# Both down projections of a two-layer trunk by seven products instead of eight

## The chip, the cores and the metric

One Trainium2 chip, one of its cores. The metric is the device time of one execution in microseconds; the kernel before was run three times. A profile is one further execution of the program, recorded by the hardware profiler, with a line for each instruction.

## The reference

One inference step of a trunk with two layers: RWKV-7 time mixing and a feed-forward part, then band attention on shared keys and values and a second feed-forward part. There are 1024 tokens of a prompt and 8 x 16 tokens of samples, so 1152 columns, and 1024 features. The change is in the last line of the feed-forward parts:

```python
D_MODEL, D_FF = 1024, 2816

def modulate(h, shift, scale):
    return h * (1.0 + scale[:, None, :]) + shift[:, None, :]

def swiglu(h, w_gate, w_up, w_down):
    return (jax.nn.silu(h @ w_gate) * (h @ w_up)) @ w_down
...
# each sub-layer: shift, scale, gate from silu(c) @ W + b
# h = modulate(rms_norm(x), shift, scale);  x = x + gate * sublayer(h)
```

The result must be good to fp32.

## The kernel before

Everything is stored with features on the 128 partitions and tokens as columns. Columns lie in two parts: part c=0 has 512, part c=1 has 640 (the last 128 of it are the samples). Every fp32 product is made of three matmuls (`mm3`, all matmuls have its line, L143): both operands are split into a high and a low half of type fp32r (`split`: ScalarE makes the high half, L272, VectorE the low one, L273), and high x high, high x low and low x high are added up in PSUM. So each weight or activation tile costs one operation on ScalarE and one on VectorE before TensorE can use it.

The gates (`gate_up`) run over 22 tiles f of 128 hidden features. For a tile, gate and up projection together are a two by two block product (weights: gate and up by the two halves of the 1024 input features; activations: the same halves by the two halves of the columns of each part), which is made with seven products instead of eight (a form of Strassen's scheme). The combined weights are made on GpSimd (`strassen_weights`, L1340 to L1343), the combined activations once per layer. Each product is twelve matmuls of 256 columns and twelve of 320 into a wide PSUM tile (two of them are named S, one PT; they are used in turn). Evictions add the products up: ScalarE copies, VectorE adds from PSUM, and three additions per tile between SBUF tiles on GpSimd (all additions have L1369). L1383 and L1385 then multiply silu(gate) and up: s0 and s1 are the tile's output for the first and second half of the columns of both parts. They are stored to DRAM (`sd`, L1390). The SBUF tiles of these steps (t, x, xin) come from one pool of 11 buffers, "e", through `ev`.

The down projection (in `ffn`) takes 11 pairs p of hidden tiles. For each pair and column part it loads the activations (`h<-sd`, L1411) into a slot of the pool h0 or h1 (14 slots each), splits them, loads and splits the weights (`rq<-in_wd`, L249, into 16 buffers `w`), and makes eight output tiles n; for each, VectorE adds the pair's product to the sum so far (L1436). The last pairs are reordered so that column part 1 ends first. The input x is added with the gate of the modulation (`residual`, L1170, which also serves the attention).

In layer 0 the modulations of the next sub-layers (16 units of four weight tiles) are computed inside the down projection: `step(7)` after each pair takes the generator `ada_steps` seven steps on, each with a load of 128 x 1024 from `wada` (L260) into a slot of h0, and four small matmuls. When a column part is complete, `done` normalizes and splits it (L1558, L1559) for the keys' and values' projection (`kv`), which begins with `nw = 4` output tiles of the keys. All DMAs of these parts are issued by SyncE's queue (SP) in one order.

The order of instructions on each engine is not written by hand. The code is written stage by stage, and a scheduler orders each engine's instructions; `issue_after` holds a group of instructions behind a given one.

Of the kernel before, what the change touches and what calls it, by code (L numbers as in the profile page):

```python
# [76 lines left out]
def prep(i):  # L77
# [68 lines left out]
class Trunk:  # L146
# [54 lines left out]
    def ada_steps(self, units, tag="aux", bufs=1, tile=None):  # L201
# [3 lines left out]
        def load(u, i):  # L205
            w = (tile or self.rawtile)()
            self.wload(w[:, :1024], self.a["wada"][u, i])
            return w
        todo = [(u, i) for u in units for i in range(4)]
        ahead = None  # L210
        for u in units:
            ps = self.bank(tag, bufs)
            for i in range(4):
# [3 lines left out]
                for q in range(4):  # L217
                    mm(nc, ps[32 * q:32 * q + 32, c], self.scT[:, i % 2 * 4 + q, :], w[:, q * 256:q * 256 + 256], i % 2 == 0, i % 2 == 1)
                if i < 3:
                    yield  # L220
            sb = (tile or self.rawtile)()[:, :512]
# [1100 lines left out]
    def strassen_weights(self, l, f, gp=None):  # L1322
# [4 lines left out]
        def put(t):  # L1327
            hi, lo = (self.wq.tile([128, 512], F32R, tag="w", name=self.nm("w"), bufs=16) for _ in range(2))
# [21 lines left out]
    def gate_up(self, sd, B, W, cs):  # L1350
# [17 lines left out]
        def add(eng, out, x, y):  # L1368
            eng.tensor_tensor(out, x, y, ALU.add)  # L1369
# [12 lines left out]
        add(gp, t5, t5, u3)  # L1382
# [3 lines left out]
        for h, s in enumerate((s0, s1)):  # L1386
            for c in cs:
                o, n = 256 * c - n0, (256, 320)[c]
                t0 = 512 * c + n * h
                nc.sync.dma_start(sd[:, t0:t0 + n], s[:, o:o + n])  # L1390

    def ffn(self, l, B, W, part1, xsrc, dst, done):

        nc = self.nc
        sd = [self.dp.tile([128, 2, 1152], F32, name=f"sd{l}_{p}") for p in range(11)]
        self.gate_up(sd[0][:, 0], B, iter(W), (0,))
        for _ in part1:
            pass
        self.gate_up(sd[0][:, 0], B, iter(W), (1,))
        for f in range(1, 22):  # L1400
            self.gate_up(sd[f // 2][:, f % 2], B, self.strassen_weights(l, f, nc.vector if f == 1 else None), (0, 1))
        self.ada = self.ada_steps(range(12, 28), "acc", 1) if l == 0 else iter(())
        gate = 48 * l + 40
        acc, end = {}, iter(())
        act, W = {}, {}

        def begin(p):
            for c in range(2):
                w = (512, 640)[c]
                raw, hi, lo = (self.slot(c, dt)[:, :2 * w].rearrange("p (i t) -> p i t", i=2) for dt in (F32, F32R, F32R))  # L1410
                nc.sync.dma_start(raw, sd[p][:, :, self.cols(c)])  # L1411
                self.split(hi, lo, raw)
                act[p, c] = hi, lo
            W[p] = [self.halves(self.a[f"wd{l}"][f]) for f in (2 * p, 2 * p + 1)]
            self.step(7)

        for p, c in [(p, c) for p in range(9) for c in range(2)] + [(9, 1), (10, 1), (9, 0), (10, 0)]:
                if (p, c) not in act:
                    begin(p)
                if p == 0:  # L1420
                    acc[c] = self.feats(c)
                if p == 10:
                    st = self.sq_open()
                for n in range(8):
                    ns = slice(n % 4 * 128, (n % 4 + 1) * 128)
                    d, parts = self.pz(c)
                    for z, o, m in parts:
                        for i in range(2):
                            wh, wl = W[p][i][n // 4]
                            hi, lo = (act[p, c][h][:, i, o:o + m] for h in range(2))  # L1430
                            self.mm3(z, wh[:, ns], wl[:, ns], hi, lo, i == 0, i == 1)
# [554 lines left out]
```

## Time and profile before

| | us |
|---|---|
| median of 3 runs | 3810.54 |
| lowest, highest | 3801.19, 3811.68 |
| the profiled execution's own time | 3804.49 |
| its span, first to last instruction | 3802.7 |
| mean granted TensorE clock | 0.940 |

| stretch of the profiled execution, us | what runs |
|---|---|
| 0 to 1290 | layer 0's time mixing |
| 1290 to 1799 | layer 0's gates |
| 1776 to 2148 | layer 0's down projection, with the modulations |
| 2143 to 2280 | keys and values |
| to 3030 | attention |
| 3030 to 3520 | layer 1's gates |
| 3520 to the end | layer 1's down projection |

Neighbouring stages overlap. In the views that follow, L is a line of the kernel, "x24" the number of instructions in a group, times are microseconds unless marked ns, and "<-" in brackets names what ended the engine's wait. A table by windows gives for each stretch its length, then busy time and count of each engine, the granted clock, the busy share of the 16 DMA engines and GB/s.

### The profile page before, as it was taken

Reading aid. Unit: us, or ns where it says so; the run is one execution under the profiler, and the core shown is the slowest. Engines: PE = TensorE matmul, PEld = TensorE weight load, DVE = VectorE, ACT = ScalarE, POOL = GpSimd, SP = SyncE. Lnnn points to the kernel's source line nnn. Section 1 sums busy time; section 2 is a strip of 40 time slices with the busy share of each in tenths; the row PEclk is TensorE's granted clock in tenths of the full one; section 3 lists DMA queues with packets and bytes.
Section 4 is the critical chain, followed back from the end, with each engine's and each line's share of the span. In section 5 each row is a group of like instructions: output and inputs, shape, how many; then the busy total and the mean of one; then the engine's idle time right before and its main releaser. Section 6 shows DMA issues by size and latency. Waiting matters only on the chain.

```text
span 3802.7 us, 72100 instructions
## 1 busy us (share of the span) xinstructions
PE 3506.1 (92%) x28550; PEld 3098.0 (81%) x28550; DVE 2263.6 (60%) x4396; ACT 1573.8 (41%) x3006; POOL 591.6 (16%) x497
## 2 busy tenths in 40 slices
PE   5889989989999799999999899789889799999999
PEld 4777778777667699999888879667677799999898
DVE  4666667765445854554457742666565755545667
ACT  5545546544223533333311452556554533333310
POOL 0000000000011154453000100000000255444000
PEclk9887899899699899999999999899899899999999
DMA  5876776776665322224654122554565322222521
GB/s 212 236 216 170 207 220 184 201 203 201 192 197 176 113 84 76 76 73 157 221 177 172 64 71 92 153 151 155 152 203 178 120 78 71 76 75 96 171 86 66
DMA packets 426995, 554.01 MB, mean 146 GB/s; under 512 B 128385, under 2 KB 292737, under 8 KB 422177
## 3 DMA queue, kind: packets, MB, share of 16 engines
q1 hardware_dynamic: 351344, 450.68, 36.9%
q0 software_dynamic: 22224, 80.36, 6.9%
q10 hardware_dynamic: 53088, 18.36, 2.1%
q8 instruction: 225, 3.69, 0.4%
q14 instruction: 114, 0.93, 0.1%
HBM read 415.85 MB, written 133.40 MB: 144 GB/s over the span
## 4 chain that ended last, share of the span: by engine, by line
PE 69%; DMA 11%; DVE 10%; issue 4%; ACT 4%; SPq 1%; ACTq 0%; POOL 0%; DVEq 0%; POOLq 0%
PE S L143 32%; PE PT L143 15%; PE acc L143 12%; PE st L143 3%; PE O L143 2%; PE G L143 1%; DVE h L273 1%; PE aux L143 1%; PE PT L1811 1%; PE Y L143 1%; DMA TT<-Z 1%; DMA h<-out_kT 1%; DVE wlo L273 1%; DMA raw<-in_rw_o 1%; DMA h<-in_wo 1%
## 5 line engine op out<-in xcount | busy, mean ns | idle before, releaser
L143 PE MATMUL S<-h,w 128*128 128x320 f32 (+1 forms) x4944 | 689.7, 298 | 12.3 <-ACT h L272 4.8
L143 PEld LDWEIGHTS S<-h,w 128*128 128x128 f32 x4944 | 671.8, 191 | 18.4 <-ACT h L272 5.6
L143 PE MATMUL S<-h,wh 128*128 128x320 f32 (+1 forms) x2844 | 529.8, 338 | 15.9 <-DVE h L1170 6.8
L143 PE MATMUL acc<-mx,whi 128*128 128x384 f32 x1728 | 508.5, 372 | 32.7 <-ACT whi L272 13.0
L143 PEld LDWEIGHTS S<-h,wh 128*128 128x128 f32 x2844 | 456.1, 189 | 70.8 <-issue 12.3
L272 ACT ACTIVATE w<-rq 128x512 fp32r<-128x512 f32 x308 | 192.6, 629 | 515.1 <-PE S L143 201.1
L143 PEld LDWEIGHTS acc<-mx,whi 128*128 128x128 f32 x1728 | 337.6, 204 | 63.3 <-ACT whi L272 16.9
L273 DVE TENSOR_TENSOR w<-rq,w 128x512 fp32r<-128x512 f32 x308 | 267.8, 872 | 199.8 <-ACT w L272 199.0
L143 PE MATMUL PT<-h,w 128*128 128x320 f32 (+1 forms) x2448 | 347.6, 297 | 10.2 <-ACT h L272 4.7
L143 PEld LDWEIGHTS PT<-h,w 128*128 128x128 f32 x2448 | 332.1, 190 | 12.2 <-ACT h L272 5.1
L143 PE MATMUL acc<-mx,wlo 128*128 128x384 f32 x864 | 316.1, 366 | 8.3 <-DVE wlo L273 8.3
L1369 POOL TENSOR_TENSOR t<-t,t 128x576 f32<-128x576 f32 (+1 forms) x132 | 226.5, 1717 | 442.2 <-ACT t L1376 320.1
L143 PE MATMUL PT<-h,wh 128*128 128x320 f32 (+1 forms) x1428 | 284.2, 342 | 8.2 <-ACT h L1558 2.3
L143 PEld LDWEIGHTS PT<-h,wh 128*128 128x128 f32 x1428 | 231.7, 188 | 38.5 <-issue 5.0
L143 PEld LDWEIGHTS acc<-mx,wlo 128*128 128x128 f32 x864 | 175.0, 203 | 20.6 <-DVE wlo L273 12.9
L273 DVE TENSOR_TENSOR wlo<-raw,whi 128x1024 fp32r<-128x1024 f32 x114 | 139.1, 1221 | 84.9 <-ACT whi L272 83.8
L272 ACT ACTIVATE wh<-rq 128x512 fp32r<-128x512 f32 x124 | 74.8, 625 | 245.1 <-PE S L143 161.4
L273 DVE TENSOR_TENSOR h<-h,h 128x1024 fp32r<-128x1024 f32 (+4 forms) x112 | 122.3, 1106 | 88.3 <-ACT h L272 72.1
L272 ACT ACTIVATE whi<-raw 128x1024 fp32r<-128x1024 f32 x114 | 119.6, 1053 | 129.0 <-PE acc L143 62.6
L272 ACT ACTIVATE h<-h 128x1024 fp32r<-128x1024 f32 (+4 forms) x112 | 103.5, 935 | 159.8 <-DMA h<-sd 111.1
L1369 DVE TENSOR_TENSOR t<-S,t 128x576 f32<-128x576 f32 (+1 forms) x116 | 86.4, 744 | 122.7 <-PE S L143 122.7
L1436 DVE TENSOR_TENSOR h<-h,S 128x640 f32<-128x640 f32 (+1 forms) x150 | 111.9, 750 | 78.9 <-PE S L143 78.7
(444 smaller groups left out, 5625.0 us busy)
## 6 DMA issues: line engine op xcount, KB each, us to landing
h<-in_wada SPq DMA_DIRECT2D x64, 512.0 KB, 6.3
rq<-in_wg SPq DMA_DIRECT2D x88, 256.0 KB, 2.6
rq<-in_wu SPq DMA_DIRECT2D x88, 256.0 KB, 2.6
rq<-in_wd SPq DMA_DIRECT2D x88, 256.0 KB, 3.1
raw<-in_wada POOLq DMA_DIRECT2D x32, 512.0 KB, 5.0
kc<-in_ck SPq DMA_DIRECT2D x16, 1024.0 KB, 5.1
vc<-in_cv SPq DMA_DIRECT2D x16, 1024.0 KB, 6.0
sd<-t SPq DMA_DIRECT2D x88, 160.0 KB, 1.9
```

The lines of the kernel that those rows point to most:

```text
L143: return nc.tensor.matmul(out, lhsT, rhs, start=start, stop=stop)
L272: self.nc.scalar.activation(hi, x, AF.Copy)
L273: self.nc.vector.tensor_tensor(lo, x, hi, ALU.subtract)
L1369: eng.tensor_tensor(out, x, y, ALU.add)
L1436: nc.vector.tensor_tensor(y, y, d, ALU.add)
L1811: nc.tensor.transpose(pt[:, j * 128:(j + 1) * 128], P[:, j * 128:(j + 1) * 128], self.C("ident"))
```

## The change

The down projection becomes a two by two block product as well, made of seven products. Its four blocks of weights are pairs of (even or odd hidden tiles) and (first or second half of the output features); those of the activations are (even or odd hidden tiles) and (first or second half of a part's columns).

- *Operands.* `down_open` gives `gate_up` a function that stores a tile's s0 and s1. At an even tile s0 is stored and both are kept; at an odd one four operations of VectorE (L1441, L1443, L1445, L1448) make the combinations, and the seven operands of the pair are stored in 14 DMAs (L1418), by product i and group j of four, four and three pairs (`Bd`).
- *Weights.* `down_sums` makes four combined blocks of weights for 1408 columns of each of four output tiles m: 32 groups per layer, one or two per hidden tile, each one load (L1458), four operations of GpSimd on 128 x 176 (L1460 to L1463) and one store (L1464). These four are held behind the gates' last addition on GpSimd (`last_add`).
- *Products.* `down` takes the products in the order 0, 1, 2, 4, 5, then 6 and 3; in layer 0 these last two come first for column part 1 and then for part 0. For each product it loads three operands per column part (L1491) and splits them; for each m it loads three pieces of weights (L1502) and makes 11 x 3 matmuls of 256 columns and as many of 320. PSUM is emptied by ScalarE's copy or VectorE's addition (L1536) into four sums, and residuals, stores and squares follow as soon as an output is complete.
- *Modulations.* A weight tile is loaded as two of 128 x 512 (`aw`, L264) from the pool e; three steps follow each m.
- *Buffers.* The weights have 14 buffers instead of 16, and the keys' projection begins with three output tiles instead of four.

```diff
-            d[f"wd{l}"] = i["w_down"][l].reshape(22, 128, 1024)
+            d[f"wd{l}"] = i["w_down"][l].reshape(11, 2, 128, 2, 4, 128).transpose(2, 3, 1, 4, 0, 5).reshape(128, 4, 5632)
...
-            self.wload(w[:, :1024], self.a["wada"][u, i])
+            n = 1024 // len(w)
+            for j, t in enumerate(w):
+                self.wload(t, self.a["wada"][u, i][:, j * n:(j + 1) * n])
...
-        self.hw = ("w", "w", 16)
+        self.hw = ("w", "w", 14)
...
-            add(gp, t5, t5, u3)
+            self.last_add = add(gp, t5, t5, u3)
...
+    def down_open(self, l):
...
+        def put(p, i, t):
+            for c in range(2):
+                nc.sync.dma_start(self.Bd[c][i][p // 4][:, p % 4], t[:, part[c]])
...
+                put(p, 2, s1)
+                nc.vector.tensor_tensor(t6, s1, e1, ALU.subtract)
+                put(p, 6, t6)
+                nc.vector.tensor_tensor(e1, e1, e0, ALU.subtract)
+                put(p, 4, e1)
+                nc.vector.tensor_tensor(e0, e0, t6, ALU.add)
+                put(p, 5, e0)
+                put(p, 1, s0)
+                nc.vector.tensor_tensor(t3, s0, e0, ALU.subtract)
+                put(p, 3, t3)
...
+    def down_sums(self, l, g):
+        m, j = divmod(g, 8)
+        q = self.wq.tile([128, 4, 176], F32, tag="ws", name=self.nm("ws"), bufs=2)
+        nc.sync.dma_start(q, self.a[f"wd{l}"][:, :, g * 176:(g + 1) * 176])
+        with self.tc.issue_after(self.last_add.ins):
+            gp.tensor_tensor(q[:, 3], q[:, 2], q[:, 3], ALU.add)
+            gp.tensor_tensor(q[:, 2], q[:, 0], q[:, 2], ALU.subtract)
+            gp.tensor_tensor(q[:, 0], q[:, 3], q[:, 0], ALU.subtract)
+            gp.tensor_tensor(q[:, 1], q[:, 1], q[:, 0], ALU.subtract)
+        nc.sync.dma_start(self.Ws[m][:, :, j * 176:(j + 1) * 176], q)
+
+    def down(self, l, xsrc, dst, done):
+        ks = [(j, k) for j, n in enumerate((4, 4, 3)) for k in range(n)]
+        turns = [(i, (0, 1)) for i in (0, 1, 2, 4, 5)]
+        if l:
+            turns += [(i, (0, 1)) for i in (6, 3)]
+        else:
+            turns += [(i, (c,)) for c in (1, 0) for i in (6, 3)]
+            part512 = lambda: self.ev("aw")[:, 0:512]
+            self.ada = self.ada_steps(range(12, 28), "acc", 1, lambda: (part512(), part512()), part512)
...
+        for i, cs in turns:
+            X = operand(i, cs)
+            for m in range(4):
+                W = weights(i, m)
+                d = self.wide()[:, 256:832]
+                for c in cs:
+                    for n, (j, k) in enumerate(ks):
+                        self.mm3(d[:, part[c]], W[j][0][:, s], W[j][1][:, s], hi, lo, n == 0, n == 10)
...
+                self.step(3)
...
-        nw = 4
+        nw = 3
```

SyncE's queue in layer 0's down projection, where the second pair's (before) and the second product's (after) activations are loaded. Here h is a slot for activations, rq a raw tile of weights, aw a modulation tile. Before:

```order
L249 DMA rq_20341<-in_wd 128x512
L249 DMA rq_20347<-in_wd 128x512
L1411 DMA h_19789<-sd_1_14100 128x2x640
L249 DMA rq_20353<-in_wd 128x512
L249 DMA rq_20604<-in_wd 128x512
L1411 DMA h_20059<-sd_2_14101 128x2x640
L260 DMA h_19865<-in_wada 128x1024
```

After:

```order
L1502 DMA rq_20716<-in_wd 128x512
L1502 DMA rq_20722<-in_wd 128x512
L1491 DMA h_20425<-bd_0_1_0_14102 128x1024
L1491 DMA h_20443<-bd_1_1_0_14123 128x1280
L264 DMA aw_20299<-in_wada 128x512
L264 DMA aw_20300<-in_wada 128x512
L264 DMA aw_20394<-in_wada 128x512
```

The modulations' loads are now twice as many, half as large, and stand in the same queue between the operands' groups.

GpSimd in the gates, from the additions of one tile to the next tile's combined weights; t are eviction tiles, ws the down projection's weights. Before:

```order
L1369 TENSOR_TENSOR t_14712<-t_14712,t_14713 128x576
L1369 TENSOR_TENSOR t_14712<-t_14712,t_14714 128x576
L1369 TENSOR_TENSOR t_14713<-t_14713,t_14715 128x576
L1340 TENSOR_TENSOR rq_15265<-rq_15200,rq_15202 128x512
L1341 TENSOR_TENSOR rq_15200<-rq_15196,rq_15200 128x512
```

After:

```order
L1373 TENSOR_TENSOR t_14774<-t_14774,t_14775 128x576
L1373 TENSOR_TENSOR t_14774<-t_14774,t_14776 128x576
L1373 TENSOR_TENSOR t_14775<-t_14775,t_14777 128x576
L1460 TENSOR_TENSOR ws_15010<-ws_15010 128x176
L1460 TENSOR_TENSOR ws_15017<-ws_15017 128x176
L1461 TENSOR_TENSOR ws_15010<-ws_15010 128x176
L1461 TENSOR_TENSOR ws_15017<-ws_15017 128x176
L1462 TENSOR_TENSOR ws_15010<-ws_15010 128x176
L1462 TENSOR_TENSOR ws_15017<-ws_15017 128x176
L1344 TENSOR_TENSOR rq_15360<-rq_15295,rq_15297 128x512
```

Four or eight sums come between the last addition and the combined weights, and some of them later among these.

VectorE at the end of a tile's evictions, after an odd tile in the new kernel; L273 (now L277) is a weight's low half. Before:

```order
L1369 TENSOR_TENSOR t_15435<-PT_15607,t_15434 128x576
L273 TENSOR_TENSOR w_15876<-rq_15682,w_15875 128x512
L1383 TENSOR_TENSOR t_15432<-t_15432,t_15433 128x576
L1369 TENSOR_TENSOR t_15435<-S_15639,t_15435 128x576
L273 TENSOR_TENSOR w_15925<-rq_15916,w_15924 128x512
L1385 TENSOR_TENSOR t_15431<-t_15431,t_15435 128x576
L273 TENSOR_TENSOR w_15955<-rq_15918,w_15954 128x512
L1369 TENSOR_TENSOR t_15671<-PT_15718,t_15670 128x576
```

After:

```order
L1387 TENSOR_TENSOR t_15539<-t_15539,t_15540 128x576
L1373 TENSOR_TENSOR t_15542<-S_15746,t_15542 128x576
L1441 TENSOR_TENSOR t_15773<-t_15539,t_15287 128x576
L277 TENSOR_TENSOR w_16004<-rq_15810,w_16003 128x512
L1389 TENSOR_TENSOR t_15538<-t_15538,t_15542 128x576
L1443 TENSOR_TENSOR t_15287<-t_15287,t_15286 128x576
L1445 TENSOR_TENSOR t_15286<-t_15286,t_15773 128x576
L277 TENSOR_TENSOR w_16065<-rq_16056,w_16064 128x512
L1448 TENSOR_TENSOR t_15774<-t_15538,t_15286 128x576
L1373 TENSOR_TENSOR t_15799<-PT_15846,t_15798 128x576
```

The four operations stand between the last eviction of the odd tile and the next tile's addition from PT.

More of the change, by code (lines that the diff above doesn't have):

```diff
@@ L1327, in put @@
         def put(t):
-            hi, lo = (self.wq.tile([128, 512], F32R, tag="w", name=self.nm("w"), bufs=16) for _ in range(2))
+            hi, lo = (self.wq.tile([128, 512], F32R, tag="w", name=self.nm("w"), bufs=self.hw[2]) for _ in range(2))
             self.split(hi, lo, t)
@@ L1348, in strassen_weights, with gate_up @@
         yield put(a22)
-    def gate_up(self, sd, B, W, cs):
+    def gate_up(self, put, B, W, cs):
         nc = self.nc
@@ L1368, in add @@
         def add(eng, out, x, y):
-            eng.tensor_tensor(out, x, y, ALU.add)
+            return eng.tensor_tensor(out, x, y, ALU.add)
         t1, s0, s1, t5, u2, u3 = (new() for _ in range(6))
@@ L1385, in gate_up @@
         dve.tensor_tensor(s0, s0, u3, ALU.mult)
[L1386 to L1390, printed above, removed]
+        put(s0, s1, cs)
     def ffn(self, l, B, W, part1, xsrc, dst, done):
         nc = self.nc
-        sd = [self.dp.tile([128, 2, 1152], F32, name=f"sd{l}_{p}") for p in range(11)]
-        self.gate_up(sd[0][:, 0], B, iter(W), (0,))
+        spill = self.down_open(l)
@@ new lines, in ffn, with first, even, f @@
+            self.gate_up(spill(f), B, self.strassen_weights(l, f, nc.vector if f == 1 else None), (0, 1))
+            for g in range(32 * (f - 1) // 21, 32 * f // 21):
+                self.down_sums(l, g)
+        return self.down(l, xsrc, dst, done)
+    def down_open(self, l):
+        nc = self.nc
+        part = (slice(0, 256), slice(256, 576))
+        self.Bd = [[[self.dp.tile([128, n, (256, 320)[c]], F32, name=f"bd{l}_{c}_{i}_{j}") for j, n in enumerate((4, 4, 3))] for i in range(7)]
+                   for c in range(2)]
+        self.Ws = [self.dp.tile([128, 4, 1408], F32, name=f"ws{l}_{m}") for m in range(4)]
+        b12 = self.dp.tile([128, 576], F32, name=f"b12_{l}")
+        held = []
+        def put(p, i, t):
+            for c in range(2):
+                nc.sync.dma_start(self.Bd[c][i][p // 4][:, p % 4], t[:, part[c]])
+        def first(s0, s1, cs):
+            c, = cs
+            nc.sync.dma_start(self.Bd[c][0][0][:, 0], s0)
+            nc.sync.dma_start(b12[:, part[c]], s1)
+        def even(p):
+            def f(s0, s1, cs):
+                put(p, 0, s0)
+                held[:] = s0, s1
+            return f
+        def odd(p):
+            def f(s0, s1, cs):
+                if p == 0:
+                    held[:] = (self.ev("t")[:, 0:576] for _ in range(2))
+                    for c in range(2):
+                        nc.sync.dma_start(held[0][:, part[c]], self.Bd[c][0][0][:, 0])
+                    nc.sync.dma_start(held[1], b12)
+                e0, e1 = held
+                t6, t3 = (self.ev("t")[:, 0:576] for _ in range(2))
+                put(p, 2, s1)
[8 more added lines that the diff above has]
+                put(p, 3, t3)
+            return f
+        return lambda f: first if f == 0 else (odd if f % 2 else even)(f // 2)
@@ L1447, in ffn @@
                     next(end, None)
-                if p == 10:
-                    for _ in end:
+            if l == 0 and i == 3:
+                for g in (self.ada, end):
+                    for _ in g:
                         pass
-                    end = done(c, acc[c], st)
+                end = done(cs[0], acc[cs[0]], sq[cs[0]])
         return end
@@ L1489, in weights @@
                         yield
-                for _ in part(0, lambda: self.wq.tile([128, 512], F32, tag="w", name=self.nm("x"), bufs=16)):
+                for _ in part(0, lambda: self.wq.tile([128, 512], F32, tag="w", name=self.nm("x"), bufs=self.hw[2])):
                     pass
```

132 lines of the change are left out of this document (86 added, 46 removed).

## The prediction

> **What bounds the kernel now.** I read the page's sums, the chain that ended last, then a table by stage of both feed-forward parts.
>
> ```profile
> PE 3506.1 (92%) x28550; PEld 3098.0 (81%) x28550; DVE 2263.6 (60%) x4396; ACT 1573.8 (41%) x3006; POOL 591.6 (16%) x497
> PE 69%; DMA 11%; DVE 10%; issue 4%; ACT 4%; SPq 1%; ACTq 0%; POOL 0%; DVEq 0%; POOLq 0%
> core 0: us, PE busy (x) PEld busy (x) DVE busy (x) ACT busy (x) POOL busy (x), PEclk, DMA share, GB/s
> 1290.00:1776.00 486.00, 478.33 (x3539) 475.09 (x3540) 268.59 (x361) 171.10 (x296) 230.21 (x146) 0.99 0.23 77
> 1776.00:1830.00 54.00, 54.00 (x386) 48.06 (x385) 16.22 (x23) 25.03 (x38) 4.61 (x3) 1.00 0.83 298
> 1830.00:1980.00 150.00, 150.00 (x1008) 122.22 (x1007) 84.16 (x117) 30.66 (x39) 0.00 (x0) 1.00 0.56 197
> 2126.00:2170.00 44.00, 34.54 (x165) 29.04 (x164) 37.10 (x73) 19.73 (x41) 7.66 (x5) 0.92 0.19 70
> 3030.00:3520.00 490.00, 485.83 (x3610) 483.95 (x3611) 265.37 (x333) 167.05 (x286) 233.92 (x148) 0.99 0.24 81
> 3600.00:3700.00 100.00, 100.00 (x575) 91.52 (x574) 66.01 (x88) 17.53 (x23) 0.00 (x0) 1.00 0.25 81
> ```
>
> Gates run at 1290–1776 and 3030–3520, the down projections at 1776–2126 and from 3520 to the end. Inside a down projection TensorE leaves no gap (150.00 of 150, 100.00 of 100) at clock 1.00: fewer columns shorten it one for one, as long as loads (0.56 of the DMA engines in layer 0, 0.25 in layer 1) and evictions keep up. In the gates TensorE has 98–99%, so what is added there on VectorE or GpSimd is free only while no eviction comes late.
>
> **Removed: TensorE columns.** Timelines of a down projection and of a gate tile give the price of a matmul from one group's start to the next.
>
> ```profile
> 1500.17 3.36 PE L143 MATMUL PT<-h,w 128*128 128x256 f32 x24
> 1503.37 6.55 PE L143 MATMUL S<-h,w 128*128 128x256 f32 x48
> 3614.97 1.92 PE L143 MATMUL PT<-h,wh 128*128 128x320 f32 x12
> 3616.72 3.68 PE L143 MATMUL S<-h,wh 128*128 128x320 f32 x24
> 3624.76 1.52 PE L143 MATMUL PT<-h,wh 128*128 128x512 f32 x6
> 3626.14 3.06 PE L143 MATMUL S<-h,wh 128*128 128x512 f32 x12
> ```
>
> 320 columns cost 1.75/12 = 0.146 us, 512 cost 1.38/6 = 0.230. A gate product is twelve of 256 and twelve of 320 columns in 3.20 us, 0.133 on average. Before, a layer's down projection has 22 feature tiles x 8 outputs x 3 = 528 matmuls of 512 and 1056 of 320: 121.4 + 154.2 = 275.6 us. After, 7 products x 4 output tiles x 11 x 3 = 924 of 256 and 924 of 320, the gates' mix: 1848 x 0.133 = 245.8. Saved 29.8 a layer, about **-60** in both. The modulations' matmuls are the same in number.
>
> **Layer 0: the loads get closer.** DMA views of 1776–2126 and, for its queue and the operand loads, 3520–3800; then two short windows.
>
> ```profile
> DMA packets 26169, 66.95 MB, mean 191 GB/s; under 512 B 2592, under 2 KB 3616, under 8 KB 26144
> q1 hardware_dynamic: 26144, 66.59, 53.7%
> h<-in_wada SPq DMA_DIRECT2D x64, 512.0 KB, 6.3
> q1 hardware_dynamic: 14807, 29.43, 31.6%
> h<-sd SPq DMA_DIRECT2D x10, 640.0 KB, 4.4
> 1780.00:1820.00 40.00, 40.00 (x287) 34.11 (x286) 12.11 (x16) 17.96 (x27) 4.61 (x3) 1.00 0.96 351
> 1780.00:1790.00 10.00, 10.00 (x77) 10.00 (x76) 5.28 (x6) 5.66 (x8) 1.07 (x1) 1.00 0.98 361
> ```
>
> A packet took 0.537 x 16 x 350 / 26144 = 115 ns at 2.55 KB, and 0.316 x 16 x 280 / 14807 = 96 ns at 1.99 KB: a line of 27 ns + 0.035 ns per byte, so 98 ns for 2 KB, 169 for 4 KB, 62 for 1 KB (estimates). The modulations' 64 loads of 4 KB rows become 128 of 2 KB: 33.6 MB, 16384 packets, 100 us of all 16 engines instead of 87. From the first of them to the last I count besides 17 MB of weights (52 us), 19 MB of operands (49) and 5 MB of x (19): 220 us of all engines. On TensorE this stretch holds the first five products and part of the sixth, 175–180 us, and the modulations' matmuls, 50–55: 228 us. Before, 0.56 was asked of the engines; now 0.96. That share was held for 40 us at a time (0.96), and 0.83 over 54 us. At 0.97 nothing stalls, at 0.83 the stretch lasts 265 us (+37), at 0.75 it lasts 293 (+65). I take 0.89, between the two rows: 247, **+20**; ends 0 and +65. Splitting those loads also doubles their issues on SP (64 more, from a queue in which operand and weight loads stand behind loads that wait for a pool buffer); of the 11 buffers there, x tiles and squares use the same.
>
> The Trainium skill, "DMA: Bandwidth & Descriptors", section "Measured", asks for transfers of 1 MiB for 75% of peak, which speaks against halving these to 256 KB. The trace shows 0.98 and 361 GB/s with transfers of 128 to 640 KB mixed, so here it is many in flight that decide. By that page's limit of about 358 GB/s on the HBM side (section "Where 436 GB/s comes from") the stretch's 74.7 MB would need 209 us, an estimate, and the term would be 0.
>
> **Layer 1** has 20 MB of weights, 23 of operands and 9 of x in 246 us: 213 GB/s, about 0.6. Its price is the start of a product: nine of ten free slots hold the running product's operands, so the next one's second and third load wait for the last output tile's matmuls, then 4.4 us of landing and two splits. With the first group of loads already there and the scheduler taking three output tiles turn about, I take 0.8 us for each of six starts: **+5** (0 to +20), in layer 0 it lies inside the stretch above.
>
> **Gates: four subtractions per two tiles on VectorE, 32 groups of four sums per layer on GpSimd.** Timeline of a tile, and one line's groups.
>
> ```profile
> 1506.23 1.30 POOL L1340 TENSOR_TENSOR rq<-rq,rq 128x512 f32<-128x512 f32 x1
> 1506.30 1.83 DVE L1383 TENSOR_TENSOR t<-t,t 128x576 f32<-128x576 f32 x1 [1.32 <-POOL t L1369]
> 1507.60 1.69 POOL L1341 TENSOR_TENSOR rq<-rq,rq 128x512 f32<-128x512 f32 x1
> 1509.76 0.74 DVE L1385 TENSOR_TENSOR t<-t,t 128x576 f32<-128x576 f32 x1
> 1509.98 1.68 POOL L1342 TENSOR_TENSOR rq<-rq,rq 128x512 f32<-128x512 f32 x1 [0.69 <-DVE w L273]
> 1510.52 1.68 DVE L273 TENSOR_TENSOR w<-rq,w 128x512 fp32r<-128x512 f32 x1
> 1516.92 0.69 DVE L273 TENSOR_TENSOR w<-rq,w 128x512 fp32r<-128x512 f32 x1 [1.91 <-ACT w L272]
> 1520.70 1.42 POOL L1369 TENSOR_TENSOR t<-t,t 128x576 f32<-128x576 f32 x1 [7.08 <-ACT t L1376]
> L1369 POOL TENSOR_TENSOR rq<-rq,rq x6: 852/1515/2327, 1300.0 to 3031.9; 128x256 f32<-128x256 f32 x6
> ```
>
> VectorE's and GpSimd's operations on two SBUF tiles don't overlap: L1383 started at 1506.30, GpSimd ended at 1507.53, L1383 0.60 later (1.83 instead of 0.74); L1342 and the split at 1510.52 show it both ways. A subtraction of 576 columns is 0.74; a sum of 176 columns, from 852 ns at 256 and 1.30 us at 512, about 0.71 (estimate). In two tiles (44.7 us) that adds 4 x 0.74 + 12.2 x 0.71 = 11.6 us, to 14 splits of 0.69, 4 products of 0.74, 6 additions of 1.42 and 8 combinations of 1.30 = 31.5: 43.1 of 44.7. Counting only what an operation still took once released (0.54, 0.60, 1.16), it is some 36. So there is room, but little; GpSimd's idle 7.08 us takes the sums. VectorE's row at the end of an odd tile is four subtractions longer, with two splits between, ahead of the eviction of the next tile's second product; I lay it out to end at 12.4–13.0 us after the tile's start, TensorE wants the bank at 12.8. I take 0.45 us per two tiles, 22 times: **+10** (0 to +45). Weights are prepared some 20 us ahead; 14 buffers instead of 16 cost 3 of these: nothing alone.
>
> The Trainium skill, "SBUF — State Buffer", section "Who interferes with whom", makes this a lock between GpSimd and a VectorE operation with two SBUF inputs; by it the sum is 43 of 44.7, near the point where the gates pay, and the rows above agree.
>
> The 14 stores per two tiles replace 8 (0.23 of the engines busy there): hidden.
>
> **Ends.** Before, TensorE stands twice for VectorE's residuals and splits at layer 0's end:
>
> ```profile
> 2132.50 1.66 PE L143 MATMUL S<-h,wh 128*128 128x512 f32 x6 [2.51 <-DVE h L1170]
> 2140.87 2.41 PE L143 MATMUL S<-h,wh 128*128 128x512 f32 x6 [3.72 <-DVE h L1170]
> ```
>
> After, VectorE still has more work than TensorE between the two column parts (the window at 2126 has it at 37.10 of 44), so the wait of about 10 us stays; the keys' first three output tiles ahead instead of four leave 24 x 2 matmuls of 320 less to fill it, 7 us, of which the fourth's, loaded later, may still fill some: **+3** (0 to +7). The very last output tile has residual, store: **+1** (-2 to +4).
>
> **Sum:** -60 + 20 + 5 + 10 + 3 + 1 = -21 against the profiled execution's own 3804.5 (span 3802.7): 3783.5. The shown median, 3810.5, lies 6 above that execution, the runs from 3801 to 3812; I give a quarter of it: **3785**. What a measurement of this kernel can't tell from no change is 0.3%, 11.4 us.
>
> **Rivals.**
> 1. *All is hidden.* Layer 0's loads hold 0.97 (the window of 40 us speaks for it, the 54 us against), gates and starts cost under 10 in all: -60 + 10 = -50, 3755 to 3765. 0.16.
> 2. *Given back in the gates.* The lock's queueing makes evictions late by 0.9–1.9 us per two tiles (for it: 43.1 of 44.7; against it: 7.08 us of GpSimd idle), +20 to +42: -11 to +11, 3800–3822, about 3808. 0.20.
> 3. *Slower: layer 0's transfers bound it.* With the other terms at -41, it is lost by over 11.4 when the stretch passes 280 us, a share under 0.785; small rows, spills landing and buffers returned late make 0.72 (the 54 us at 0.83 had larger rows): 305 us, +77, in all +36, about 3845. Against it: 351 GB/s over 40 us. 0.16.
>
> **How the numbers follow.** The forecast, a gain of 12 to 42 (3768–3798), has 0.48. Faster 0.48 + 0.16 = 0.64; same 0.20; slower 0.16. The range takes rival 2 whole and most of rival 1: 3750 to 3822.
>
> **What would show it.** Right: down projections of about 246 us in layer 1 from the first product to the last, some 20 longer in layer 0 beyond the modulations' matmuls, DMA share near 0.9 there, TensorE's waits put down to loads of weights or operands; gates of 488–492 us, with some idle time before a second product's first matmul. Wrong: gates over 500 us with TensorE released by VectorE's evictions (rival 2); a layer-0 stretch of 280 us or more (rival 3); share of 0.96 and no waits (rival 1); or a matmul price in the long runs of one PSUM tile other than 0.133.

## The result, and the profile after

The changed kernel's median is 3787.3 us (3780.2 to 3793.9, six runs) against 3806.5 for the kernel before (3801.2 to 3821.9, six runs): ratio 0.9945, interval 0.9929 to 0.9960. The forecast was 3785. The profiled execution of the changed kernel has a span of 3783.6 us; that of before had 3802.7.

First the page's sums and its chain that ended last; then the table by windows, with the columns of the prediction's table. Its rows are 440 us of the gates in either layer, layer 0's stretch with the modulations, that layer's down projection as a whole, its end, and three pieces of layer 1's down projection: its first four output tiles (the first product), the next seven, and the last seventeen with the tail (a tile is 66 matmuls).

```profile
PE 3457.2 (91%) x29078; PEld 3088.6 (82%) x29078; DVE 2248.3 (59%) x4380; ACT 1667.9 (44%) x3182; POOL 769.7 (20%) x743
PE 65%; DMA 13%; DVE 10%; issue 6%; ACT 4%; SPq 1%; POOL 1%; ACTq 0%; DVEq 0%; POOLq 0%
...
1360.00:1800.00 440.00, 440.00 (x3310) 440.00 (x3309) 258.13 (x297) 144.33 (x238) 299.53 (x253) 1.00 0.46 147
3060.00:3500.00 440.00, 440.00 (x3309) 440.00 (x3308) 260.26 (x298) 142.95 (x237) 307.72 (x258) 1.00 0.45 143
1822.70:2078.00 255.30, 252.48 (x2018) 217.11 (x2016) 120.67 (x208) 99.51 (x161) 0.00 (x0) 1.00 0.86 297
1807.30:2285.70 478.40, 453.18 (x3191) 392.18 (x3190) 255.04 (x466) 213.52 (x390) 9.76 (x9) 0.98 0.62 210
2097.00:2165.00 68.00, 56.51 (x366) 52.35 (x366) 50.67 (x117) 34.11 (x70) 0.00 (x0) 0.90 0.39 121
3518.20:3554.60 36.40, 35.47 (x265) 35.06 (x263) 18.18 (x21) 10.33 (x20) 10.57 (x9) 1.00 0.77 252
3554.60:3629.20 74.60, 66.93 (x463) 65.79 (x463) 37.88 (x53) 31.71 (x45) 0.00 (x0) 0.93 0.66 219
3629.20:3783.60 154.40, 149.68 (x1124) 149.42 (x1122) 84.86 (x155) 49.49 (x77) 0.00 (x0) 1.00 0.50 160
```

TensorE works 48.9 us less (3506.1 to 3457.2), not 60. The gates take every microsecond of TensorE (440.00 of 440) although GpSimd is busy for 300 us of it. Where TensorE stands or runs slower is in layer 0's down projection and in the second and third product of layer 1's (66.93 busy of 74.60, granted clock 0.93, for seven tiles).

For before, the row of the whole down projection of layer 0, from its first matmul to the values' projection that follows:

```profile
1797.30:2289.60 492.30, 474.14 (x2927) 395.11 (x2926) 288.39 (x489) 159.99 (x280) 15.74 (x10) 0.99 0.42 147
```

So of 29.8 us fewer columns TensorE's busy time shows 21.0 (474.14 to 453.18), and its idle time grew from 18.2 to 25.2: the stage gained 13.9.

Four marks in each trace cut the span for a ledger: g0, layer 0's first gate matmul; V, the values' projection after layer 0; g1, layer 1's first gate matmul; the end.

| us | start to g0 | g0 to V | V to g1 | g1 to end |
|---|---|---|---|---|
| before | 1290.6 | 999.0 | 716.7 | 796.3 |
| after | 1299.9 | 985.9 | 718.4 | 779.4 |
| difference | +9.3 | -13.1 | +1.7 | -16.9 |

The first column has the same work in both. In the profiled executions of this study that contain the old layer 0 it was 1290.6, 1297.1 and 1315.2, in those with the new one 1299.9 to 1320.9. It varies more between executions than the change is worth, so below the runs are compared stage by stage, and the whole time by medians on one chip. The other columns vary too. From g0 to V it was 998.3 to 999.1 in three executions with the old layer 0, and 983.3 to 992.2 in six whose layer 0 is that of the changed kernel. From V to g1 it was 713.1 to 716.7 in those three, and 718.3 to 727.5 in all eleven that have the new layer 0 in some form.

### The profile page after: what moved, and what is told of

It is laid out like the page before. It is cut to its first block, busy times and chain, and to the rows that moved or that the text cites. A ratio compares the mean times of both kernels' runs of the same rounds, so it can differ in the third digit from the quotient of the medians.

```text
span 3783.6 us, 74619 instructions
## 1 busy us (share of the span) xinstructions
PE 3457.2 (91%) x29078; PEld 3088.6 (82%) x29078; DVE 2248.3 (59%) x4380; ACT 1667.9 (44%) x3182; POOL 769.7 (20%) x743
## 4 chain that ended last, share of the span: by engine, by line
PE 65%; DMA 13%; DVE 10%; issue 6%; ACT 4%; SPq 1%; POOL 1%; ACTq 0%; DVEq 0%; POOLq 0%
PE S L143 30%; PE PT L143 14%; PE acc L143 12%; PE st L143 3%; PE O L143 2%; DMA raw<-in_rw_o 1%; DVE h L277 1%; PE G L143 1%; PE PT L1937 1%; PE aux L143 1%; DMA TT<-Z 1%; DVE wlo L277 1%; DMA bt<-in_rel 1%; DMA xin<-x 1%; DMA h<-bd 1%
## 5 line engine op out<-in xcount | busy, mean ns | idle before, releaser
L143 PE MATMUL S<-h,w 128*128 128x256 f32 (+1 forms) x7374 | 1036.6, 299 | 23.9 <-ACT h L276 7.4
L143 PEld LDWEIGHTS S<-h,w 128*128 128x128 f32 x7374 | 1002.4, 191 | 46.2 <-issue 19.1
L276 ACT ACTIVATE w<-rq 128x512 fp32r<-128x512 f32 (+1 forms) x500 | 304.4, 614 | 661.4 <-PE S L143 290.0
L277 DVE TENSOR_TENSOR w<-rq,w 128x512 fp32r<-128x512 f32 (+1 forms) x500 | 384.4, 773 | 286.6 <-ACT w L276 247.9
L143 PE MATMUL PT<-h,w 128*128 128x256 f32 (+1 forms) x3714 | 532.0, 298 | 10.2 <-DVE h L277 3.8
L143 PEld LDWEIGHTS PT<-h,w 128*128 128x128 f32 x3714 | 506.4, 190 | 20.5 <-issue 7.8
L277 DVE TENSOR_TENSOR h<-h,h 128x1024 fp32r<-128x1024 f32 (+6 forms) x152 | 169.3, 1125 | 121.2 <-ACT h L276 111.2
L276 ACT ACTIVATE h<-h 128x1024 fp32r<-128x1024 f32 (+6 forms) x152 | 142.8, 950 | 147.8 <-DMA h<-bd 110.0
L143 PEld LDWEIGHTS acc<-mx,wlo 128*128 128x128 f32 x864 | 174.1, 202 | 21.6 <-DVE wlo L277 13.9
L277 DVE TENSOR_TENSOR wlo<-raw,whi 128x1024 fp32r<-128x1024 f32 x114 | 139.0, 1221 | 83.6 <-ACT whi L276 82.7
L276 ACT ACTIVATE whi<-raw 128x1024 fp32r<-128x1024 f32 x114 | 119.6, 1053 | 128.7 <-PE acc L143 61.6
L143 PE MATMUL S<-h,wh 128*128 128x320 f32 (+1 forms) x744 | 148.5, 348 | 12.7 <-DVE h L1685 4.7
L143 PEld LDWEIGHTS S<-h,wh 128*128 128x128 f32 x744 | 123.4, 195 | 31.3 <-ACT wh L276 6.3
```

Of the source, the lines that this page charges most:

```text
L143: return nc.tensor.matmul(out, lhsT, rhs, start=start, stop=stop)
L276: self.nc.scalar.activation(hi, x, AF.Copy)
L277: self.nc.vector.tensor_tensor(lo, x, hi, ALU.subtract)
```

## The experiments

**Does the gates' lock cost anything?** The first run does each group of four sums twice (leaving the values as they are), which puts GpSimd beyond what the prediction thought the lock would bear.

```
 (in down_sums, after the four sums)
+for k in range(4):
+    gp.tensor_tensor(q[:, 1], q[:, 1], q[:, 0], ALU.subtract if k % 2 else ALU.add)
```

> Behind each group's four sums on GpSimd four more of the same size (alternately adding and subtracting, so the values stay but for rounding): 128 more per layer at about 0.57 us. The changed kernel's gates lose nothing (22.37 us a tile as before). Counted by full durations VectorE's two-SBUF operations and GpSimd's take 41.4 of 44.7 us per two tiles in the changed kernel, 48.3 here: a tile would then take 24 us and the two layers' gates 75 us more. Counted by what an operation takes once the other is done (0.54, 0.60, 1.16 us) they take some 35 and 41: the tile stays at 22.4, and nothing is lost but some microseconds at the end of each layer's gates.

Measured, one profiled execution (3808.5 us): the window inside layer 0's gates, and the sums' group of the changed kernel.

```profile
1360.00:1800.00 440.00, 440.00 (x3310) 440.00 (x3309) 287.61 (x298) 142.25 (x237) 382.43 (x369) 1.00 0.46 144
```

```profile
L1460 POOL TENSOR_TENSOR ws<-ws x64: 557/566/1281, 1359.9 to 3521.4; 128x176 f32<-128x176 f32 x64
```

TensorE still has no gap. GpSimd (382) and VectorE (288) together are recorded busy for 670 us of 440; 242 of VectorE's are operations on two SBUF tiles, so these and GpSimd's make 624, more than the time there. As such operations hold each other up (the prediction's rows of 1.83 instead of 0.74 us), their recorded durations contain waiting, and no eviction came late. The same group in the doubled kernel shows it:

```profile
L1460 POOL TENSOR_TENSOR ws<-ws x64: 563/1028/1480, 1369.7 to 3545.4; 128x176 f32<-128x176 f32 x64
```

Its median grew from 0.566 to 1.028 us, and VectorE's 139 splits of weights from 117.0 to 154.5 us, with no delay on TensorE. A sum alone is 0.566 us, not 0.71. From g0 to the first matmul behind layer 0's gates it was 506.6 us before, 507.4 after and 507.0 with the sums doubled. So the gates cost under 1 us, also with twice the sums.

**One layer at a time.** Both kernels keep the old form, with the old layout and 16 weight buffers, in the other layer (`if l in (1,):` or `if l in (0,):` around the new spill, sums and down projection).

> Layer 1 by seven products, layer 0 as before (16 weight buffers and four key tiles there, modulations' loads as before). By the two profiles layer 1's part is worth 282.4 - 265.5 = 17 us: 3806 - 17 = 3789, ratio 0.9955. If the whole gain is layer 1's, ratio 0.9945; if the two layers' parts were equal shares of the measured 21 us, 0.997.

> Layer 0 by seven products with all that belongs to it, layer 1 as before. By the two profiles, from the first gate matmul to the values' projection, it is worth 999.1 - 985.9 = 13 us: 3793, ratio 0.9965. But the changed kernel's profile also reached its first gate matmul 9 us later than before, in a stage whose instructions and order are the same; if that is a cost of the change (and not the spread of single executions), it shows here or in the layer 1 kernel as a first gate matmul at about 1300 instead of 1291, and one of them is worth only 4 to 8 us.

Layer 1 alone: 3801.3 against 3817.6 us, ratio 0.9961 (0.9945 to 0.9978). Layer 0 alone: 3820.0, ratio 1.0002 (0.9991 to 1.0013). In their traces layer 1's stage went from 796.3 to 779.9 in the first; in the second g0 to V went from 999.0 to 989.2, but V to g1 came out at 721.9 instead of 716.7. Beside each other on their chip, the kernel with the new layer 0 gains 9.1 us from g0 to V (989.2 against 998.3) and loses 8.8 from V to g1 (721.9 against 713.1). All that can be measured of the gain comes from layer 1; what layer 0 gains in its own stage doesn't reach the whole time, because it is lost again behind it.

The kernel before was profiled once more for its stages:

> The kernel before once more, for its stages in a second execution. The time mixing ahead of the first gate matmul took 1291 us in the first profile and 1300 to 1315 in the profiles of kernels that leave it as it is. If that is the spread of executions, it lies above 1295 here too, while the stages after it agree within 4 us with the first profile (999 from the first gate matmul to the values' projection, 717 to layer 1's gates, 796 to the end). If the change had cost it, it is 1291 again.

They were 1297.1, 998.3, 715.9 and 795.4: the three after g0 repeat within 1 us. And the changed kernel, on the chip of a later experiment:

> The changed kernel once more, on the chip of the next run. By the stages of the profiles so far the change is worth 13 us in layer 0 (999.0, 998.3, 998.3 with the old one; 985.9, 983.3, 989.2 with the new) and 17 in layer 1, less 2 to 5 between them: 25 to 28, ratio 0.993; measured was 0.9945 (0.9929 to 0.996). If the time mixing ahead of the gates, whose code is the same, is slower with the change (1300 to 1321 in profiles with the new layer 0; 1291, 1297 and 1315 without), the ratio stays at 0.9945 to 0.996 and the first gate matmul comes after 1300 here too; if not, 0.992 to 0.994.

It had 3801.2 against 3817.1 us there, ratio 0.9959 (0.9944 to 0.9974), and stages of 987.3, 724.6 and 776.9.

**What stands at layer 1's product starts.** TensorE's timeline of the changed kernel shows the first product's last tile and the second's start, the second row being one matmul that waited 3.45 us, then the third product's start and later rows without waits; S and PT are the PSUM tiles. Below it, SP's queue at the second product's start (L1502 loads weights, L1529 x, L1491 operands), and what SP's weight loads waited for from 3518 to 3620, then from 3518 to 3551.

```profile
3545.70 8.95 PE L143 MATMUL S<-h,w 128*128 128x256 f32 x66
3558.10 0.58 PE L143 MATMUL S<-h,w 128*128 128x256 f32 x1 [3.45 <-ACT h L276]
3559.36 2.72 PE L143 MATMUL S<-h,w 128*128 128x256 f32 x11 [0.68 <-DVE h L277]
3561.88 2.34 PE L143 MATMUL PT<-h,w 128*128 128x256 f32 x10
...
3607.68 0.39 PE L143 MATMUL PT<-h,w 128*128 128x256 f32 x1 [2.28 <-ACT h L276]
3608.67 6.26 PE L143 MATMUL PT<-h,w 128*128 128x256 f32 x32 [0.49 <-DVE h L277]
3629.24 8.95 PE L143 MATMUL PT<-h,w 128*128 128x256 f32 x66
3655.62 8.95 PE L143 MATMUL PT<-h,w 128*128 128x256 f32 x66
```

```profile
3545.25 4.45 SPq L1529 DMA_DIRECT2D xin<-x  x9
3549.79 0.85 SPq L1502 DMA_DIRECT2D rq<-in_wd  x2
3550.70 0.90 SPq L1491 DMA_DIRECT2D h<-bd  x2
...
3552.31 2.23 SPq L1491 DMA_DIRECT2D h<-bd  x3
3562.02 0.81 SPq L1502 DMA_DIRECT2D rq<-in_wd  x2
3562.93 0.38 SPq L1491 DMA_DIRECT2D h<-bd  x1
```

```profile
SPq L1502 <- DVE w L277: 39.3, 17, 8.5
SPq L1502 <- DVE w L277: 3.9, 2, 3.5
```

The matmuls wait for the operand's split (h, L276 and L277), and the split for loads that SP issued at 3550.7, 32.6 us after the down projection began, behind the gates' last stores, 22 x tiles and the weights. Of the 39.3 us that weight loads waited for buffers only 3.9 lie ahead of that; but the product's sixth and last operand load went out at 3562.93, behind weights that had waited. Two theories: the operands' place in the queue is what is late; or the pace of the buffers is, whatever stands there.

The first kernel issues the next product's operands two output tiles earlier, in both layers:

```
-for i, cs in turns:
-    X = operand(i, cs)
+X = None
+for n_turn, (i, cs) in enumerate(turns):
+    X = operand(i, cs) if X is None else Xn
 ...
+        if m == 2 and n_turn + 1 < len(turns):
+            Xn = operand(*turns[n_turn + 1])
```

> The next product's operand loads are written two output tiles earlier, so that they stand ahead of the last weight loads in SyncE's queue; nothing else changes. In the changed kernel's profile layer 1's down projection takes 265.5 us from its first matmul to the end of the span; 28 output tiles of 8.79 us are 246.1, the end after the last matmul 4.9, and 14.5 are lost, nearly all at the starts of the second and third products (7.7 us idle, the rest matmuls at a lower clock behind the idle time). Theory 1 (the place in the queue: the loads are issued at 3550.7, when TensorE needs them at 3554.5): those starts lose under 3 us, layer 1's down projection takes 252 to 256, the median falls by 10 to 15 from 3787 to about 3775. Rival (slots: nine of ten free slots are taken, so the second and third operands can't come before the running product's last matmuls): the starts keep 6 us or more each, the median stays within 5 of 3787.

The second takes the x tiles out of SP's queue in layer 1:

```
-nc.sync.dma_start(x[:, part[c]], xsrc[:, f, at])
+(nc.gpsimd if l else nc.sync).dma_start(x[:, part[c]], xsrc[:, f, at])
```

> In layer 1 the loads of x for the residuals are issued from GpSimd's queue instead of SyncE's. 22 of them stand ahead of the second product's operands. If they are what delays the operands (about 0.5 us of SyncE's time each), the loads are issued 5 to 10 us earlier and the start of the second product loses nothing: median 3787 - 5 to -8. If the weight loads' wait for their buffers sets the queue's pace, the x loads only fill waiting time: the operands are issued at most 3 us earlier and the median stays within 3 of 3787.

Operands ahead: 3791.8 against 3817.6 us, ratio 0.9925 (0.9908 to 0.9943), layer 1's stage 767.4, as expected of the place in the queue. By the ratios that is some 8 us better than the change, less than the 10 to 15 expected: layer 0's stage came out at 996.3, 4 us above the highest of the six with the changed kernel's layer 0, in one execution. X tiles elsewhere: 3795.8 us, ratio 0.9947 (0.9928 to 0.9965), stage 776.5; the operands went out 30.2 us after the start instead of 32.6, and the waits were 6.0 us instead of 7.7. So it is the place in the order of issue, and not the x tiles alone: with them gone the weights ahead of the operands waited longer (5.6 us for buffers instead of 3.9, and 4.4 for other transfers), and the operands gained only 2.4 us. The next kernel does it in layer 1 alone (`if l and m == 2 ...`).

> The operand loads two output tiles earlier in layer 1 alone, and the counter of the PSUM tiles as in the changed kernel. Against the run of the changed kernel beside it: layer 1's stage 764 to 768 instead of 775 to 780, so 11 to 14 us or 0.3 to 0.37% faster. From the attention's last statistics to layer 1's first gate matmul 71.5 to 72.1 as in the changed kernel, if that is the counter's position (67 to 68 in the run that moved it); 68 if it is the order of loads.

Measured beside the unedited change (3801.2 us): 3790.5, ratio to before 0.9935 (0.9919 to 0.9950), stage 766.9. Layer 1's first four output tiles, the next eight (the second and third product whole) and the last sixteen with the tail, and SP's queue:

```profile
3534.70:3571.20 36.50, 35.81 (x270) 35.61 (x269) 22.89 (x25) 13.57 (x22) 10.44 (x9) 1.00 0.81 280
3571.20:3641.50 70.30, 70.27 (x528) 70.01 (x527) 37.13 (x55) 31.72 (x50) 0.00 (x0) 1.00 0.75 245
3641.50:3788.20 146.70, 140.83 (x1057) 140.57 (x1056) 79.69 (x150) 45.43 (x71) 0.00 (x0) 0.99 0.49 155
```

```profile
3551.74 0.88 SPq L1491 DMA_DIRECT2D h<-bd  x2
3552.71 1.35 SPq L1502 DMA_DIRECT2D rq<-in_wd  x3
3554.11 1.95 SPq L1529 DMA_DIRECT2D xin<-x  x4
```

The operands go out 17.0 us after the start (3551.74 - 3534.7); TensorE has no gap in the second and third product (70.27 of 70.30) at clock 1.00. The down projection took 253.5 us, against 265.5 in the change and 263.4 in its repeat.

**Are layer 0's loads what costs there?** The same number of modulation loads, half their bytes; each loaded column is used twice, so this kernel leaves out half of the modulations' weights:

```
 (in the load of two halves)
+self.wload(t[:, :256], self.a["wada"][u, i][:, j * n:j * n + 256])
+return [t[:, :256] for t in w for o in range(2)]
```

> Each modulation tile of 128 x 512 is loaded as 128 x 256, and its columns are used twice (so the modulations aren't the reference's): 16.8 MB less in layer 0's down projection, the same instructions else. If the transfers cost layer 0 something (0.84 of the engines over 278 us, some gaps behind loads), it gets 5 us or more shorter from the first gate matmul to the values' projection, below 981 against 986. If they are hidden, it stays within 3 us of 986, and the waits at the first modulation tile (1.5 to 1.9 us) are all that goes.

Then the full loads at another rate per output tile, `self.step(4)` and `self.step(2)` for `self.step(3)`:

> Layer 0's modulations are taken four steps on behind each output tile instead of three, so their 128 loads are asked for within 16 output tiles instead of 21. In the changed kernel's profile they take from 1822.7 to 2071.9, and the queue's packets fill 0.851 of 256 us there, 218 us of all engines, as counted (220). Theory: it is the length of this stretch that kept the transfers nearly hidden; with 16 tiles TensorE has 16 x 8.79 + 55 = 196 us of work for some 190 of transfers, so it waits for loads: from the first gate matmul to the values' projection 5 to 20 us more than 986. Rival: transfers cost nothing at that share either: within 4 us of 986.

> Two steps instead of three: the modulations reach into the last products of column part 1, and eight steps of 64 are left for its end. Theory (transfers cost layer 0 about 11 us at 0.85, as with half the modulations' bytes, 975 against 986): a longer stretch at a lower share wins some of it, 978 to 983 from the first gate matmul to the values' projection, unless the rest at the end of column part 1 waits for its last loads, which would give it back (within 4 of 986).

Half the bytes: g0 to V 974.7 us, 11.2 less than the change's 985.9 and below all six executions with its layer 0 (whole time 3796.2, ratio 0.9932, 0.9910 to 0.9955). Four steps: 987.5, no difference (3803.5 against 3811.9 us, one run each). Two steps: 1012.7, 27 more (3822.8 us). TensorE's longest waits there from 2080 to 2165, the four steps' stretch, and with half the bytes the stretch and then the whole down projection of layer 0:

```profile
PE acc L143 <- DMA aw<-in_wada: 7.5, 6, 3.0
```

```profile
1840.00:2055.00 215.00, 212.01 (x1675) 170.88 (x1673) 78.24 (x128) 73.96 (x120) 0.00 (x0) 1.00 0.86 298
```

```profile
1843.00:2099.00 256.00, 251.41 (x2054) 219.99 (x2054) 123.65 (x221) 101.09 (x167) 0.00 (x0) 1.00 0.74 236
1828.30:2295.50 467.20, 443.36 (x3191) 389.09 (x3189) 253.63 (x466) 211.86 (x389) 9.50 (x9) 0.99 0.56 180
```

With half the bytes the share falls from 0.86 to 0.74 and about 11 us come back. Of these only 1.4 are idle time of TensorE (23.8 us against 25.2); 9.8 are busy time (443.36 against 453.18). So the loads cost TensorE something that the view of waits hardly shows. A part is a change of order: where loads come later, the groups of small matmuls stand singly between the products instead of in a row (51 runs of them in the change's stretch, 39 here). Counted from start to start, the last small matmul ahead of a product takes 0.31 us and a product's matmul of 320 columns ahead of a small one 0.24 instead of 0.15; by these figures 12 runs more are some 4 us, an estimate. With four steps the stretch is 215 instead of 255 us at the same share and rate (0.86, 298 GB/s against 297), and the stage is not longer: asking for the loads sooner cost nothing. Whether 0.86 was the limit of the transfers these runs don't tell. With two steps the rest of the modulations is left to the end of column part 1, ahead of the keys and values, and TensorE waits there for their loads.

**A counter that nobody meant to change.** From the first `S<-h,kc` matmul of the attention's end to g1 the three kernels with the old layer 0 took 100.3, 100.7 and 99.6 us, ten with the new one 104.1 to 107.1 (106.6 in the change), with the same 548 or so matmuls. Three PSUM tiles are handed out in turn by one counter; layer 0's down projection now advances it 36 times instead of 176, which leaves another remainder by three (0 instead of 2), so all that follows gets other banks. The last kernel has the operands ahead in layer 1, and moves the counter by two, to 38 with the old remainder, at the end of layer 0's down projection (`if l == 0: self.nwide += 2`):

> Operand loads two output tiles earlier in layer 1 alone, and the counter that hands out the three wide PSUM tiles moved on by two behind layer 0's down projection, so that the attention meets it as before the change (176 uses in layer 0's down projection before, 36 now). Theory: the loads are worth 12 us as in the profile with both layers (779.4 to 767.4), without the 10 us that they cost in layer 0 there; the counter's position is worth 5 us, since from the attention's last statistics to layer 1's first gate matmul it was 66.0 and 66.6 in the two kernels with the old layer 0, and 71.6 to 72.1 in the four with the new: 3787 - 17 = 3770 where the changed kernel has 3787, ratio 0.990. Rival: that difference is the order of loads or the 14 buffers and stays at 72: ratio 0.9915.

TensorE's waits for VectorE's evictions in that piece, of before, of the change, and of this kernel:

```profile
PE PT L143 <- DVE h L1170: 1.2, 1, 1.2
```

```profile
PE PT L143 <- DVE h L1174: 5.2, 3, 2.2
```

```profile
PE PT L143 <- DVE h L1174: 1.4, 1, 1.4
```

And the three windows, in that order, then that of the kernel with the operands ahead in layer 1 and the counter left alone:

```profile
2906.10:3006.35 100.25, 86.73 (x548) 79.42 (x547) 60.69 (x107) 40.85 (x80) 16.20 (x16) 0.94 0.48 156
```

```profile
2897.50:3004.20 106.70, 91.81 (x550) 82.85 (x547) 61.16 (x108) 40.99 (x80) 15.08 (x16) 0.91 0.45 149
```

```profile
2918.10:3020.15 102.05, 86.90 (x551) 79.30 (x547) 61.32 (x108) 42.32 (x82) 16.08 (x16) 0.95 0.49 159
2917.00:3021.27 104.27, 88.74 (x548) 80.63 (x547) 61.00 (x109) 40.98 (x80) 15.05 (x16) 0.94 0.48 153
```

Two of the three waits are gone, TensorE's busy time is back at 86.90, and the piece is 102.05 us instead of 106.70. All idle time together is not less (15.15 against 14.89), so what came back is busy time: the same matmuls at a clock of 0.95 instead of 0.91. The fourth row is the nearest comparison, since only the counter differs: all three waits are there, but the piece is 104.27 us at clock 0.94. In the ten executions with the counter left alone the three waits (4.8 to 6.3 us in all) went with clocks of 0.90 to 0.95 and 88.5 to 91.7 us busy. So the move is worth 2 to 5 us; that it acts by the clock alone isn't shown. Counted from the attention's last statistics to g1 it is 68.0 us with the counter moved, about 72 in the kernel of the fourth row and 70.3 to 72.9 in all ten, so it isn't the order of loads, which those two share. It is one execution of this edit. Whole time 3782.0 against 3820.2 us, ratio 0.9906 (0.9889 to 0.9923): the lowest of all, its interval below the change's own. What the counter alone adds to that isn't separated: the kernel of the fourth row has 0.9935 (0.9919 to 0.9950), and V to g1 as a whole was 726.8, not below the others (718 to 728), since the attention ahead varies.

## Why the prediction was right, and where its terms were not

The total held: -21 forecast against the profiled execution, -19.1 in the spans, 19.2 between the medians. So did the layers: the terms give -2 for layer 0 (-29.8 + 20 + 5 + 3) and -19 for layer 1 (-29.8 + 5 + 5 + 1), measured alone ratio 1.0002 (about +1 us) and 0.9961 (about -15). But some terms were off, in opposite directions, and layer 0 comes out near zero for another reason than the sum has: its own stage gained more, and that was lost behind it.

1. **Columns, -29.8 a layer: right.** An output tile is 8.79 us (3629.24 to 3655.62 are three), 28 are 246.1, forecast 245.8. With operands ahead the whole of layer 1's down projection is 253.5, with its tail of about 5.
2. **Gates, +10: wrong, it is under 1.** The step that failed is counting whole durations on VectorE and GpSimd (43.1 of 44.7 us) and laying out the eviction as late. With the sums doubled TensorE still had 440.00 of 440. The lower count in the prediction, what an operation takes once released (36), is the one that the runs allow. Rival 2 falls with it. The prediction's table also ends layer 0's gates at 1776; their last matmuls run to 1797.3, so the 486 us behind its sign "gates of 488–492 us" are 506.6 from g0, and its row at a DMA share of 0.83 is in part gates.
3. **Layer 1's starts, +5: mis-sized, 14.5.** The place was right (operands of the next product behind other loads), the size not: layer 1's down projection took 265.5, less 246.1 and 4.9 of tail. From first product to last that is 260.6 us, where the prediction's sign was about 246. Half of the 14.5 is waiting, 7.7 us, over two starts, the second product's and the third's, rather than six. Most of the rest is matmuls on a slower clock, which the term left out: after the wait of 3.45 us eleven matmuls of 256 columns took 2.52 us (3559.36 to 3561.88), 0.23 each, while later rows have 66 in 8.95, 0.14 each at most. The seven tiles in 74.60 us, at 8.79 each 61.5, have clock 0.93, 7.7 us of waits and 5.4 of slower matmuls; with the operands ahead the clock is 1.00 and both are gone. The Trainium skill, "TensorE: Matmul & The Clock Gate", section "What's actually happening", says the clock halves after an idle window of some 3.4 us; this row agrees. At the third product's start the waits were shorter, 2.28 and 0.49 us with two matmuls between, and the matmuls behind them were slower as well (32 in 6.09 us, 0.19 each). The granted clock behind either:

```profile
3557.60:3564.40 6.80, 5.62 (x24) 5.33 (x25) 5.72 (x7) 6.25 (x10) 0.00 (x0) 0.50 0.78 300
3608.80:3612.20 3.40, 3.40 (x15) 3.40 (x16) 1.16 (x1) 1.00 (x1) 0.00 (x0) 0.50 0.55 211
```

4. **Layer 0's loads, +20: probably too high, and the stretch badly sized.** It lasted 255 us, not 228 plus stalls: it holds more than the first five and a half products. The loads' 220 us of all engines were right (85.1% of 256 us is 218). Halving the modulations' bytes gave back 11 us, about the least that all of them cost; visible waits for them were only 1.46 and 0.19 us ahead of the first groups:

```profile
1825.48 0.62 PE L143 MATMUL acc<-aw,scT 128*32 128x256 f32 x4 [1.46 <-DMA aw<-in_wada]
1828.13 0.63 PE L143 MATMUL acc<-aw,scT 128*32 128x256 f32 x4 [0.19 <-DMA aw<-in_wada]
```

   The stage gained 13.1 of 29.8 us; less some 4 for the ends, 13 are left in this pair for all that the loads and the new order cost, and 10 to 20 over the six executions, where the sum has 20. Rival 3 did not come about: the share was 0.86 over 255 us, and over 215 us in another kernel, with TensorE busy for 252.48 of 255.30. Part of it isn't waiting: TensorE's busy time fell by 21.0 instead of 29.8. Counted from one matmul's start to the next in both traces, the products' matmuls, with those of the keys and values, fell by 25.6, and the small ones (modulations, squares, values) grew by 4.9.
5. **Ends.** The end of layer 0's down projection has 11.5 us of idle time (68.00 - 56.51) against 10.3 before (43.00 - 32.70), at clock 0.90 against 0.92. With 56.5 x 0.10 against 32.7 x 0.08 for the clock that is about +4, an estimate; forecast +3. Before:

```profile
2117.00:2160.00 43.00, 32.70 (x138) 26.11 (x137) 39.87 (x77) 19.78 (x37) 7.66 (x5) 0.92 0.20 71
```

6. **Not in the sum: from V to g1, +2 to +14.** The prediction took everything outside the two feed-forward parts as unmoved. The counter is 2 to 5 of it; the rest is open.

Gates 10 too high and, in this pair, loads some 7 too high were made up for by starts 9.5 too low and by what is lost from V to g1: the total was right partly by luck. Luck has a share in the spans' -19.1 too, since it holds the 9.3 us by which the changed kernel's profiled execution came later to g0.

Open: the time from the start to g0, equal in code, was 9 to 30 us longer in the executions with the new layer 0 than in before's first. One with the old layer 0 had 1315.2, and three with the new one on its chip 1307.7 to 1308.1, so it isn't that layer's code alone; whether it is spread between executions only wasn't settled. Nor was what else makes V to g1 longer behind the new layer 0, so that its gain doesn't reach the whole time, nor why operands ahead in layer 0 gave 996.3 there.

## What to carry to other kernels

When a stage is shortened, look at where the loads of the *next* piece stand in their in-order queue: behind many other loads, some of which wait for a buffer, they go out as late as those. Issuing them two tiles earlier was worth 10.7 us beside the change's own 15.9 on the same chip, by the medians. A wait of TensorE of two to four us costs more than its length: here 7.7 us of waits at two starts came with 5.4 of slower matmuls. Read a stage's cost from its length and not from its waits alone; in layer 0 most of what the loads cost was counted as busy time. And if tiles are handed out by a shared counter, count its uses before and after the change: stages that no line of the diff touches get other banks.

## What the runs showed of the hardware that was not expected

Recorded durations of VectorE and GpSimd that add up to more than the time there (624 of 440 us for operations on SBUF tiles alone, with the sums doubled) did not delay TensorE at all; waiting for the shared access is inside those durations (the same sum 0.566 or 1.028 us). The Trainium skill, "SBUF — State Buffer", section "Who interferes with whom", describes an exclusive lock; these rows show that its price can't be read by adding the durations up.

And short waits were enough for the slower clock: behind 2.28 and 0.49 us with two matmuls between, the granted clock was 0.50 for 3.40 us. What several such waits cost differs between executions: in the attention's end the same three waits, of 3.2 us or less, went with granted clocks of 0.90 to 0.95 and with 88.5 to 91.7 us of busy time for the same matmuls.
